# Expert products of a pair in unbroken runs, and tiles placed by the width of the matmuls that read them

## The chip, the cores and the metric

The kernel runs on one core of a Trainium2 chip. The metric is device time in microseconds of one execution; the median of several runs counts. The core's engines work from queues of their own: TensorE (PE, matmuls, with its weight loads as PEld), VectorE (DVE), ScalarE (ACT), GpSimd (POOL) and SyncE (SP), which issues the transfers here.

## What is computed

A network of three blocks on 512 tokens of width 1024. Two blocks (the loop over `l`) each hold stick-breaking attention, differential attention, a gated merge, a mixture of 32 experts and a gated addition of a side input; the third (`hybrid`, `ffn`) holds dilated, block-wise and recurrent branches and a dense feed-forward part. The change bears on the expert part:

```python
def expert_block(args):                    # a block of the tokens sent to expert e
    xb, e = args
    hid = jax.nn.silu(xb @ w_gate[e]) * (xb @ w_up[e])
    return hid @ w_down[e]
ys = lax.map(expert_block, (xs, blk_e)).reshape(P, D)
ys = ys * slot_gate[:, None]               # each token goes to two experts
out = jax.ops.segment_sum(ys, slot_tok, num_segments=N + 1)[:N]
```

## The kernel before

**Dense matmuls.** A float32 product is made of three float32r matmuls (high x high, high x low, low x high; `mm3`, lines 269 to 274). `wload` and `wcut` (242 to 259) load 512 KB of weights into a tile of tag `raw` and split it into two tiles of tag `wh`. `proj_f` streams 512 columns of the normalised activations (tag `f16`) against stationary `wh`; `add_out` and the end of `ffn` stream 256 columns of `wh` against stationary tiles of `q`, `o`, `g` or `tmp`; `proj_v` and others stream `wh` against stationary `f16`.

**Places.** A pool lays its tags out one after the other, in the order of their first use; all buffers of a tag follow one another. In each partition the tiles of `q`, `raw`, `wh` and `o` begin at a multiple of 128 bytes, and those of `tmp`, `f16`, `g`, `X` and `wu` 64 bytes past one.

**The expert stage** (`moe`, 908 to 1180, once for each `l`). Experts go in groups of two, 64 token places each: 16 groups, and a 17th with one expert more. A step is two matmuls side by side, one for each expert, in either half of TensorE's columns (64 of 128), each in plain float32. Group g has 8 steps `up` (gate and up product) and 4 steps `dn` (down product). The list `steps` is up 0, up 1, dn 0, up 2, dn 1 and so on, one entry a step. Other pieces are put between steps by `at(s, ...)`, in full-width matmuls or transposes:

- `gather_oh(u, tt)` (983): VectorE writes a slice of the one-hot tile OH(u) (tag `g`) for groups 2u and 2u+1; four slices, two operations each;
- `gather_rows(u, kk)` (1014): 16 matmuls that select rows, into a PSUM tile `z`, then a copy into X(u); `gather_gates(u)` (996): 8 small matmuls into `tp`, then five small VectorE operations;
- `back(u, p)` (1028): four transposes of OH(u) into `tp`, copied to OHT(u) (tag `g`);
- `hidden(g)` (1051): two transposes of the hidden values into `tp`, and a copy that `dn` g reads;
- `combine` (1070): four matmuls of OHT with the split product rows Y (tag `q`) into the one PSUM tile `o`, then an addition on VectorE that empties it; 56 of them, for 7 pairs of groups, 4 token tiles and 2 halves.

A piece that ends in an evacuation returns a function, which is put into the step after (lines 1160 to 1163). After `up`, `gate` runs on ScalarE and VectorE; after `dn`, `rows` copies on ScalarE and subtracts on VectorE. `manual_schedule` (1158) keeps the order as written in each queue of PE, ACT, DVE and POOL. Tags have fixed numbers of buffers: in this stage `g` has 4, `X` 2, `wu` (incoming weights) 5; of PSUM, `z` and `mm` have 2, `tp` and `o` have 1. A tile that finds no free buffer makes its first writer wait until the last reader of another one has ended.

In these indices, with 12 steps a group, OH(u) is written at steps 24u-25 to 24u-22 and last read at 24u-5; OHT(u) is written at 24u-6 and 24u-4 and read by additions up to step 24u+54.

Of the kernel before, what the change touches and what calls it, by code (L numbers as in the profile page):

```python
# [22 lines left out]
EARLY = dict(then=0, rope=-30, cut=20, norm=0, trans=0, route=0, fold=0, y=0, gather=0, hs=0, dma=0)  # L23
RAW, WHL, NWU = 4, 6, 5
HT = 4
LM, LH, LF = 1, 1, 3

GAT = (-25, -24, -23, -22, -9, -15, -13, -11, -9)
BAT = (-7, -5)
CAT = (40, 2)  # L30
ROPE_FREQ = (1.0, 0.1939227432012558, 0.03760603070259094, 0.007292664609849453, 0.0014142135623842478,
# [76 lines left out]
class Kern:  # L108
    def __init__(self, ctx, tc, A, out, dbg=None, stop=None):
        self.tc, self.nc, self.A, self.out = tc, tc.nc, A, out  # L110
        self.dbg, self.stop = dbg or {}, stop
        self.n = 0
        self.const = ctx.enter_context(tc.tile_pool(name="const", bufs=1))
        self.sb = ctx.enter_context(tc.tile_pool(name="sb", bufs=1))
        self.ps = ctx.enter_context(tc.tile_pool(name="ps", bufs=1, space=PSUM))
        self.dr = ctx.enter_context(tc.tile_pool(name="dr", bufs=1, space=bass.MemoryType.DRAM))
        self.ph = None
        ctx.callback(lambda: self.ph.close())
        self.phase("mix")
# [4 lines left out]
    def phase(self, name):  # L124

        if self.ph is not None:
            self.ph.close()
        self.ph = ExitStack()
        self.n += 1
        self.phsb = self.ph.enter_context(self.tc.tile_pool(name=f"{name}{self.n}", bufs=1, reuse_waits="tile"))  # L130
        self.phbufs = dict(self.PHASES[name])

    def ring(self, tag, shape, dt):

        return self.t(tag, shape, dt, bufs={"raw": RAW, "wh": WHL}[tag])


    def t(self, tag, shape, dt=F32, bufs=None):
        self.n += 1
        if tag in self.phbufs:  # L140
            return self.phsb.tile(shape, dt, tag=tag, name=f"{tag}_{self.n}", bufs=self.phbufs[tag])
        return self.sb.tile(shape, dt, tag=tag, name=f"{tag}_{self.n}", bufs=bufs)
# [98 lines left out]

    def wload(self, src, a, b, eH="act", eL="dve"):
# [4 lines left out]
        return self.wcut(raw, a, b, eH, eL)  # L247

# [3 lines left out]

    def wcut(self, raw, a, b, eH="act", eL="dve"):

        h, l = (self.ring("wh", [128, a, b], F32R) for _ in range(2))
# [219 lines left out]
    def proj_v(self, hT, w, cols, r):  # L475

        wc = [self.wload(self.wk(w, cols, kh), 4, 256) for kh in range(2)]
        for tp in range(2):
# [13 lines left out]
    def proj_f_halves(self, hT, w, c0, r):  # L492

        r += [self.mmps([128, S]) for _ in range(2)]
        wc = [self.wload(self.wk(w, c0, kh), 4, 256) for kh in range(2)]
        for half in range(2):
# [411 lines left out]
    def moe(self, l, xs):  # L908
# [9 lines left out]
        for g, tags in ((0, ("raw", "raw", "wh", "wh")), (1, ("q",) * 4)):  # L918
            for c in range(4):
                for i in range(2):  # L920
                    t = self.t(tags[c], [128, 2, 2, 256], F32, bufs={"raw": RAW, "wh": WHL, "q": 12}[tags[c]])
# [7 lines left out]
        for g in range(NG + 1):  # L929
            if g < NG:  # L930
                up[g] = len(steps)
                steps += [("up", g, j) for j in range(4 * ne(g))]
            if g > 0:
                if g == NG:
                    steps += [None] * 2
                dn[g - 1] = len(steps)
                steps += [("dn", g - 1, j) for j in range(2 * ne(g - 1))]
        N = len(steps)
# [17 lines left out]
        def load_in():  # L956
            if way_in:
# [4 lines left out]
                for k in range(4):  # L962
                    IN[g, i, 4 * h + k] = t[:, :, k]
                free = up[g] + (4 * h + 3 if ne(g) == 2 else 2 * h + 1)
                loads.setdefault(free, []).append(load_in)

        def load_out():
            if way_out:
                g, k, i = way_out.pop(0)
                tag = out_tags[nout[0] % 10]  # L970
                nout[0] += 1
                t = OUT[g, i, k] = self.t(tag, [128, 1024], F32, bufs={"raw": RAW, "wh": WHL}[tag])
                nc.sync.dma_start(t, weights(g, i)[2][k * 128:k * 128 + 128])
                loads.setdefault(dn[g] + (2 * k + 1 if ne(g) == 2 else 1), []).append(load_out)

# [38 lines left out]
        def gather_rows(u, kk):  # L1014
# [80 lines left out]
        def work(s):  # L1095

            kind, g, j = steps[s]
            two = ne(g) == 2
            if kind == "up":
                if j == 0:  # L1100
                    PS["a", g] = self.mmps([128, 2, 256])
                pa, X = PS["a", g], Xs[g // 2]
                for i in range(2):
                    k, e = (j, i) if two else (2 * j + i, 0)
                    x0 = (g % 2 * 2 + e) * 64
                    mm(pa[64 * i:64 * i + 64], X[:, k, x0:x0 + 64], IN.pop((g, e, k)), start=j == 0, stop=j == 4 * ne(g) - 1)
                if j == 4 * ne(g) - 1:
                    if two:
                        at(s + 1, lambda: gate(g, 0))
                        at(s + 2, lambda: gate(g, 1))  # L1110
                    else:
                        at(s + 1, lambda: folded("a", g, pa.rearrange("p j c -> p (j c)"),
                                                 lambda: (gate(g, 0), gate(g, 1))))
                    at(max(s + 4, dn[g] - HT), lambda: hidden(g))
            else:
                if j == 0:
                    PS["y", g] = self.pst("z", [128, 1024], 2)
                py = PS["y", g]
                for i in range(2):
                    k, q, e = (j // 2, j % 2, i) if two else (i, j, 0)  # L1120
                    cs = slice(q * 512, q * 512 + 512)
                    mm(py[64 * i:64 * i + 64, cs], HID[g][:, k, 64 * e:64 * e + 64], OUT[g, e, k][:, cs],
                       start=k == 0 or not two, stop=k == 1 or not two)
                if j == 2 * ne(g) - 1:
                    if two:
                        at(s + 1, lambda: rows(g, 0))
                        at(s + 2, lambda: rows(g, 1))
                    else:
                        at(s + 1, lambda: folded("y", g, py, lambda: (rows(g, 0), rows(g, 1))))
            for f in loads.pop(s, ()):  # L1130
                f()

        for u in range(1, 9):
            for tt in range(4):
                at(24 * u + GAT[tt], lambda u=u, tt=tt: gather_oh(u, tt))
            at(24 * u + GAT[4], lambda u=u: gather_gates(u))
            for kk in range(4):
                at(24 * u + GAT[5 + kk], lambda u=u, kk=kk: gather_rows(u, kk))
        for u in range(9):
            for p in range(2 if u < 8 else 1):  # L1140
                at(max(24 * u + BAT[p], 2 + p), lambda u=u, p=p: back(u, p))
        for j in range(7):
            for x in range(8):
                at(min(CAT[0] + 24 * j + CAT[1] * x, N + x - 8), lambda j=j, x=x: combine((2 * j, 2 * j + 1), x // 2, x % 2))
        self.moe_overflow(l, xs, hs, G, it, oe)
# [9 lines left out]
        gather_gates(0)()  # L1155
        self.moe_blocks(oe, it)
        ET = mybir.EngineType
        with self.tc.manual_schedule(engines={ET.PE, ET.Activation, ET.DVE, ET.Pool}):
            for s in range(N + 8):
                for f in todo.pop(s, ()):  # L1160
                    f = f()
                    if callable(f):
                        at(s + 1, f)
                if s in (3, 7) and s < N:
                    for _ in range(4):
                        loads.setdefault(s, []).append(load_out)
                if s < N and steps[s]:
# [139 lines left out]
    def ple(self, l, xs, then=None):  # L1307
# [3 lines left out]
        for c in range(4):  # L1311
            wc = [self.wload(self.wk(A["w_ple_gate"][l], c * 256, kh), 4, 256) for kh in range(2)]
            for tt in range(4):
# [136 lines left out]
    def dilated(self, hT, w):  # L1450
# [4 lines left out]
        for g in range(3):  # L1455
# [11 lines left out]
            for kh in range(2):  # L1467
                wc = self.wload(self.wk(w, 1536 + g * 256, kh), 4, 256)
                for tt in range(4):
# [377 lines left out]
```

## Time and profile before

| | |
|---|---|
| median of 3 runs | 2871.1 us (2870.6 to 2871.26) |
| the profiled execution | 2876.8 us, span 2875.1 us |
| TensorE busy / weight loads | 2716.9 us (94%) / 2025.3 us (70%) |
| VectorE, ScalarE, GpSimd busy | 1379.6 us (48%), 969.4 us (34%), 318.6 us (11%) |
| granted clock, mean | 0.967 of 2.4 GHz |
| moved | 383.57 MB, mean 133 GB/s |

The share of busy time is a mean over stages; the windows show single ones. Rows of the lines view give busy time and count of a group of like instructions, the mean of one, and the engine's idle time before them with what ended it. A timeline row is a series of like instructions with its start. A matmul's own duration overlaps the next one's, so work is read from starts to starts. A float32 matmul stands as two instructions in it, so a step of an expert product counts 4.

### The profile page before, as it was taken

Reading aid. Unit: us, or ns where it says so; the run is one execution under the profiler, and the core shown is the slowest. Engines: PE = TensorE matmul, PEld = TensorE weight load, DVE = VectorE, ACT = ScalarE, POOL = GpSimd, SP = SyncE. Lnnn points to the kernel's source line nnn. Section 1 sums busy time; section 2 is a strip of 40 time slices with the busy share of each in tenths; the row PEclk is TensorE's granted clock in tenths of the full one; section 3 lists DMA queues with packets and bytes.
Section 4 is the critical chain, followed back from the end, with each engine's and each line's share of the span. In section 5 each row is a group of like instructions: output and inputs, shape, how many; then the busy total and the mean of one; then the engine's idle time right before and its main releaser. Section 6 shows DMA issues by size and latency. Waiting matters only on the chain.

```text
span 2875.1 us, 37304 instructions
## 1 busy us (share of the span) xinstructions
PE 2716.9 (94%) x14791; PEld 2025.3 (70%) x14791; DVE 1379.6 (48%) x2585; ACT 969.4 (34%) x1752; POOL 318.6 (11%) x346
## 2 busy tenths in 40 slices
PE   7899996999999999999699999899999899999998
PEld 6777785544558777789444546877886677877798
DVE  6677536233347567643633336654235812533323
ACT  4555322111124445532111114544343622322222
POOL 0221001000000022010100000210001543011101
PEclk9989997999999989999799999999999999999999
DMA  5112234788853211133688872322112233233222
GB/s 170 45 37 74 81 120 150 292 302 289 294 192 103 74 45 52 59 98 123 222 312 287 296 289 96 118 74 66 52 45 70 74 99 114 81 95 96 91 90 70
DMA packets 224771, 383.57 MB, mean 133 GB/s; under 512 B 19658, under 2 KB 162599, under 8 KB 224592
## 3 DMA queue, kind: packets, MB, share of 16 engines
q1 hardware_dynamic: 224592, 381.13, 39.7%
q8 instruction: 119, 1.95, 0.3%
q14 instruction: 60, 0.49, 0.1%
HBM read 374.23 MB, written 6.85 MB: 133 GB/s over the span
## 4 chain that ended last, share of the span: by engine, by line
PE 44%; DVE 4%; ACT 1%; POOL 1%; issue 1%; POOLq 0%; DVEq 0%; ACTq 0%
PE mm L272 8%; PE mm L274 8%; PE mm L273 8%; PE z L911 5%; PE mm L911 4%; PE o L911 2%; PE z L272 1%; PE z L274 1%; PE z L273 1%; PE o L524 1%; DVE tmp L345 1%; PE o L1440 1%; PE z L1429 0%; PE z L1427 0%; DVE tmp L1595 0%
## 5 line engine op out<-in xcount | busy, mean ns | idle before, releaser
L240 DVE TENSOR_TENSOR wh<-raw,wh 128x1024 fp32r<-128x1024 f32 (+1 forms) x251 | 304.2, 1214 | 476.6 <-ACT wh L227 474.3
L272 PE MATMUL mm<-f,wh 128*128 128x512 f32 x1264 | 508.0, 404 | 3.2 <-DVE q L238 2.1
L273 PE MATMUL mm<-f,wh 128*128 128x512 f32 x1264 | 508.0, 402 | 0.0
L274 PE MATMUL mm<-f,wh 128*128 128x512 f32 x1264 | 506.5, 401 | 0.1
L227 ACT ACTIVATE wh<-raw 128x1024 fp32r<-128x1024 f32 (+1 forms) x278 | 290.4, 1046 | 505.8 <-PE mm L273 350.1
L272 PEld LDWEIGHTS mm<-f,wh 128*128 128x128 f32 x1264 | 239.7, 190 | 66.9 <-issue 6.3
L274 PEld LDWEIGHTS mm<-f,wh 128*128 128x128 f32 x1264 | 240.2, 190 | 56.5 <-issue 2.0
L273 PEld LDWEIGHTS mm<-f,wh 128*128 128x128 f32 x1264 | 240.1, 190 | 54.3 <-issue 2.2
L911 PE MATMUL mm<-wu,X 128*64 128x512 f32 x928 | 229.2, 606 | 0.0
L911 PEld LDWEIGHTS z<-g,o 128*128 128x128 f32 x1152 | 141.2, 192 | 51.0 <-issue 14.6
L911 PE MATMUL z<-g,o 128*128 128x256 f32 (+1 forms) x1152 | 154.2, 288 | 10.8 <-DVE g L994 10.8
L911 PEld LDWEIGHTS o<-q,g 128*128 128x128 f32 x448 | 75.4, 188 | 104.4 <-issue 56.8
L484 PE MATMUL mm<-wh,f 128*128 128x256 f32 x960 | 137.8, 297 | 6.0 <-ACT f L386 3.1
L911 PE MATMUL o<-q,g 128*128 128x512 f32 x448 | 134.7, 422 | 3.3 <-DVE q L1078 3.3
L484 PEld LDWEIGHTS mm<-wh,f 128*128 128x128 f32 x960 | 127.3, 200 | 11.5 <-ACT f L386 4.8
L1078 DVE TENSOR_TENSOR q<-q,o 128x512 f32<-128x512 f32 x112 | 76.6, 684 | 108.7 <-PE o L911 108.7
L911 PEld LDWEIGHTS mm<-wu,X 128*64 128x64 f32 x928 | 55.5, 136 | 87.3 <-issue 79.2
L272 PE MATMUL mm<-wh,q 128*128 128x256 f32 x384 | 112.1, 292 | 3.7 <-ACT q L227 3.7
L274 PE MATMUL mm<-wh,q 128*128 128x256 f32 x384 | 110.0, 286 | 2.4 <-POOL q L240 2.2
L273 PE MATMUL mm<-wh,q 128*128 128x256 f32 x384 | 109.3, 285 | 0.0
L273 PE MATMUL mm<-wh,f 128*128 128x256 f32 x352 | 106.1, 301 | 0.8 <-DVE wh L240 0.8
L274 PE MATMUL mm<-wh,f 128*128 128x256 f32 x352 | 106.0, 301 | 0.6 <-DVE f L387 0.6
(432 smaller groups left out, 4732.7 us busy)
## 6 DMA issues: line engine op xcount, KB each, us to landing
raw<-in_w_in_dram SPq DMA_DIRECT2D x142, 512.0 KB, 3.6
wu<-in_w_exp_gate_dram SPq DMA_DIRECT2D x116, 512.0 KB
wu<-in_w_exp_up_dram SPq DMA_DIRECT2D x116, 512.0 KB, 8.4
wh<-in_w_exp_down_dram SPq DMA_DIRECT2D x76, 512.0 KB, 6.2
raw<-in_w_exp_down_dram SPq DMA_DIRECT2D x56, 512.0 KB, 6.1
raw<-in_w_gu_dram SPq DMA_DIRECT2D x44, 512.0 KB, 3.4
raw<-in_w_down_dram SPq DMA_DIRECT2D x20, 512.0 KB, 3.5
raw<-in_w_o_dram SPq DMA_DIRECT2D x16, 512.0 KB, 5.2
```

Of the source, the lines that this page charges most:

```text
L227: nc.scalar.activation(o, i, AF.Copy, scale=scale)
L240: e.tensor_sub(o, i, h)
L272: mm(ps, aH, bH, start=first, stop=False, skip_group_check=True)
L273: mm(ps, aH, bL, start=False, stop=False, skip_group_check=True)
L274: mm(ps, aL, bH, start=False, stop=last, skip_group_check=True)
L345: self.nc.vector.scalar_tensor_tensor(h.rearrange("t k p -> t p k"), x.rearrange("t (p k) -> t p k", k=8), r, gb.rearrange("t (p k) -> t p ...
L484: self.nc.tensor.matmul(ps[:, t], hT[k // 4][:, x, k % 4, sl], wc[k // 4][y][:, k % 4], start=t + x + y + k == 0, stop=x == 1 and k == 7, ...
L524: self.nc.tensor.matmul(po, v[kt // 2][:, x, kt % 2, vc], w[y][:, kt, :], start=x + y + kt == 0, stop=y == 1 and kt == nk - 1, skip_group_ ...
L911: mm = lambda *a, **k: nc.tensor.matmul(*a, **k, skip_group_check=True)
L1078: return lambda: v.tensor_add(xs[tt][:, cs], xs[tt][:, cs], po)
L1440: nc.tensor.matmul(po[:, m, qt % 2], v[:, qt - prev + j, vc], pT[:, m, j], start=m == 0 and j == 0 and qt % 2 == 0, stop=j == prev, skip_g ...
```

## The change

1. **Runs.** An entry of `steps` is a whole product: all steps of `up` g, or of `dn` g, follow one another. The list has 35 entries (before 201): up g is step 2g-1, dn g is 2g+2. Pieces stand between products, and evacuations come right behind their matmuls, no longer a step later.
2. **Places in the list.** In one step: gates first, then the first half's `combine`, gathers and transposes, the second half's `combine`, then one-hot slices. OH(u) is written in steps 4u-6 and 4u-5; gathers of u are in 4u-4 to 4u-1, its transposes in 4u-2 and 4u-1; additions for groups 2u and 2u+1 in 4u+6 to 4u+9. All copies into X go to ScalarE.
3. **Places in memory.** Pads move tags: then `q` and `g` begin 64 bytes past a multiple of 128, and `raw`, `o`, `tmp`, `f16` at one. `wh` has slots of 4608 bytes and begins at a multiple, or 64 past one (`skip=64`) where it streams against `f16` or in `proj_f_halves`.
4. **Buffers.** `wu` has 6; the scratch for GpSimd's transfers (none are issued there) falls from 16 KB to 1 KB a partition.

```diff
-RAW, WHL, NWU = 4, 6, 5
+RAW, WHL, NWU = 4, 6, 6
...
+    def ring(self, tag, shape, dt, skip=0):
+        if tag == "raw":
+            return self.t(tag, shape, dt, bufs=RAW)
+        o = skip // 4
+        t = self.t(tag, [128, 1152], dt, bufs=WHL)[:, o:o + int(np.prod(shape[1:]))]
...
+    PADS = {("sb", "q"): 320, ("sb", "raw"): 192, ("mix", "tmp"): 64, ("mix", "f16"): 256, ("mix", "g"): 320, ("moe", "g"): 128}
     def t(self, tag, shape, dt=F32, bufs=None):
         self.n += 1
+        pad = self.PADS.get((self.phname if tag in self.phbufs else "sb", tag), 0)
+        if pad and (tag in self.phbufs, tag) not in self.padded:
+            self.padded.add((tag in self.phbufs, tag))
+            pool = self.phsb if tag in self.phbufs else self.sb
+            self.nc.gpsimd.memset(pool.tile([128, pad // 4], F32, name=f"pad_{self.n}")[:, 0:1], 0.0)
...
-        wc = [self.wload(self.wk(w, cols, kh), 4, 256) for kh in range(2)]
+        wc = [self.wload(self.wk(w, cols, kh), 4, 256, skip=64) for kh in range(2)]
...
-                steps += [("up", g, j) for j in range(4 * ne(g))]
+                steps.append(("up", g))
             if g > 0:
                 if g == NG:
-                    steps += [None] * 2
+                    steps.append(None)
                 dn[g - 1] = len(steps)
-                steps += [("dn", g - 1, j) for j in range(2 * ne(g - 1))]
+                steps.append(("dn", g - 1))
...
-            return lambda: self.copyH(Xs[u][:, kk * 2:kk * 2 + 2, 0:n], pz[:, :, 0:n], "act" if kk % 2 == 0 else "dve")
+            return lambda: nc.scalar.copy(Xs[u][:, kk * 2:kk * 2 + 2, 0:n], pz[:, :, 0:n])
...
+                n = 4 * ne(g)
+                for j in range(n):
+                    for i in range(2):
+                        k, e = (j, i) if two else (2 * j + i, 0)
+                        x0 = (g % 2 * 2 + e) * 64
+                        mm(pa[64 * i:64 * i + 64], X[:, k, x0:x0 + 64], IN.pop((g, e, k)), start=j == 0, stop=j == n - 1)
+                    for f in loads.pop((s, k), ()):
+                        f()
+                if two:
+                    gate(g, 0)
+                    gate(g, 1)
...
+                at(max(s + 2, dn[g] - 1) + (not two), lambda: hidden(g))
...
+        for u in range(1, 9):
+            at(max(4 * u - 3, 1), lambda u=u: gather_gates(u))
+        def back_rows(y):
+            for j in range(7):
+                for x in range(4):
+                    at(min(4 * j + 6 + x, N), lambda j=j, x=x: combine((2 * j, 2 * j + 1), x, y))
+        back_rows(0)
+        for u in range(9):
+            for x in range(4):
+                if u:
+                    at(max(4 * u - 4 + x, 1), lambda u=u, x=x: gather_rows(u, x))
+                if x < 2 and 2 * u + x < NG:
+                    at(max(4 * u - 2 + x, 1 + x), lambda u=u, x=x: back(u, x))
+        back_rows(1)
         for u in range(1, 9):
             for tt in range(4):
-                at(24 * u + GAT[tt], lambda u=u, tt=tt: gather_oh(u, tt))
...
+                at(4 * u - 6 + tt // 2, lambda u=u, tt=tt: gather_oh(u, tt))
...
                 for f in todo.pop(s, ()):
                     f = f()
                     if callable(f):
-                        at(s + 1, f)
+                        f()
...
-    nc = _bacc.Bacc("TRN2", target_bir_lowering=False, num_devices=1)
+    nc = _bacc.Bacc("TRN2", target_bir_lowering=False, num_devices=1, dynamic_dma_scratch_size=1024)
```

## Rows read from the trace of the kernel before

**Rows 1.** Busy time of each engine (the page's first part).
```profile
PE 2716.9 (94%) x14791; PEld 2025.3 (70%) x14791; DVE 1379.6 (48%) x2585; ACT 969.4 (34%) x1752; POOL 318.6 (11%) x346
```

**Rows 2.** Windows: stretch, length, busy PE PEld DVE ACT POOL, PEclk, DMA share, GB/s.
```profile
600.00:700.00 100.00, 100.00 (x504) 49.58 (x500) 33.25 (x70) 13.74 (x24) 0.00 (x0) 1.00 0.82 285
```

**Rows 3.** Waits, 500 to 860 us: engine, line, releaser: total, times, longest.
```profile
PEld tp L1036 <- ACT g L1037: 0.8, 1, 0.8
...
PE o L911 <- DVE q L1078: 1.6, 1, 1.6
```

**Rows 4.** Waits of SyncE's queue in the same stretch.
```profile
SPq L961 <- PE mm L911: 149.9, 27, 7.5
```

**Rows 5.** TensorE's timeline in the first expert stage: start, busy, line, tiles, count.
```profile
509.24 0.66 PE L1036 MATMUL tp<-c_all,g 128*128 128x128 f32 x4
...
512.33 3.60 PE L911 MATMUL mm<-wh,X 128*64 128x512 f32 x16
515.76 1.03 PE L911 MATMUL mm<-q,X 128*64 128x512 f32 x4
...
662.17 1.21 PE L911 MATMUL o<-q,g 128*128 128x512 f32 x4
663.31 1.94 PE L911 MATMUL mm<-wu,X 128*64 128x512 f32 x8
665.18 1.21 PE L911 MATMUL o<-q,g 128*128 128x512 f32 x4
...
848.11 1.19 PE L911 MATMUL z<-q,g 128*128 128x512 f32 x4
```

**Rows 6.** VectorE's timeline: start, busy, line, operation, tiles, [idle before].
```profile
660.30 1.23 DVE L240 TENSOR_TENSOR q<-z,q 128x1024 fp32r<-128x1024 f32 x1 [3.01 <-ACT q L227]
661.44 0.68 DVE L1078 TENSOR_TENSOR q<-q,o 128x512 f32<-128x512 f32 x1
...
664.03 0.35 DVE L993 TENSOR_SCALAR g<-c_all,small 128x256 fp32r<-128x256 f32 x1
...
664.81 0.35 DVE L993 TENSOR_SCALAR g<-c_all,small 128x256 fp32r<-128x256 f32 x1
```

**Rows 7.** TensorE's timeline at two waits, and a window behind each.
```profile
2289.07 0.50 PE L272 MATMUL mm<-o,wh 128*128 128x512 f32 x1 [3.24 <-ACT o L227]
...
2434.43 0.58 PE L272 MATMUL mm<-wh,q 128*128 128x256 f32 x1 [3.69 <-ACT q L227]
...
2289.50:2292.90 3.40, 3.18 (x8) 2.51 (x8) 2.67 (x4) 1.61 (x3) 2.34 (x1) 0.51 0.01 3
2432.80:2439.60 6.80, 5.05 (x22) 4.75 (x23) 0.42 (x1) 1.14 (x3) 2.18 (x2) 0.50 0.25 81
```

**Rows 8.** TensorE's timeline: first and last of four unbroken series.
```profile
2321.11 0.39 PE L272 MATMUL mm<-o,wh 128*128 128x512 f32 x1
...
2331.79 0.39 PE L274 MATMUL mm<-o,wh 128*128 128x512 f32 x1
2332.02 0.39 PE L272 MATMUL mm<-f,wh 128*128 128x512 f32 x1
...
2365.39 0.39 PE L274 MATMUL mm<-f,wh 128*128 128x512 f32 x1
...
2800.63 0.28 PE L272 MATMUL z<-wh,q 128*128 128x256 f32 x1
...
2812.03 0.28 PE L274 MATMUL z<-wh,q 128*128 128x256 f32 x1
...
2823.67 0.28 PE L272 MATMUL z<-wh,g 128*128 128x256 f32 x1
...
2828.99 0.28 PE L274 MATMUL z<-wh,g 128*128 128x256 f32 x1
```

**Rows 9.** Costliest groups (the page's fifth part): tiles and counts of two.
```profile
L272 PE MATMUL mm<-f,wh 128*128 128x512 f32 x1264 | 508.0, 404 | 3.2 <-DVE q L238 2.1
...
L272 PE MATMUL mm<-wh,q 128*128 128x256 f32 x384 | 112.1, 292 | 3.7 <-ACT q L227 3.7
```

More of the change, by code (lines that the diff above doesn't have):

```diff
@@ L23 @@
 EARLY = dict(then=0, rope=-30, cut=20, norm=0, trans=0, route=0, fold=0, y=0, gather=0, hs=0, dma=0)
-RAW, WHL, NWU = 4, 6, 5
-HT = 4
+RAW, WHL, NWU = 4, 6, 6
 LM, LH, LF = 1, 1, 3
-GAT = (-25, -24, -23, -22, -9, -15, -13, -11, -9)
-BAT = (-7, -5)
-CAT = (40, 2)
 ROPE_FREQ = (1.0, 0.1939227432012558, 0.03760603070259094, 0.007292664609849453, 0.0014142135623842478,
@@ L116, in __init__ @@
         self.dr = ctx.enter_context(tc.tile_pool(name="dr", bufs=1, space=bass.MemoryType.DRAM))
-        self.ph = None
+        self.ph, self.padded = None, set()
         ctx.callback(lambda: self.ph.close())
@@ L130, in phase @@
         self.phsb = self.ph.enter_context(self.tc.tile_pool(name=f"{name}{self.n}", bufs=1, reuse_waits="tile"))
-        self.phbufs = dict(self.PHASES[name])
-    def ring(self, tag, shape, dt):
-        return self.t(tag, shape, dt, bufs={"raw": RAW, "wh": WHL}[tag])
+        self.phbufs, self.phname = dict(self.PHASES[name]), name
+        self.padded = {x for x in self.padded if not x[0]}
+    def ring(self, tag, shape, dt, skip=0):
[3 more added lines that the diff above has]
+        t = self.t(tag, [128, 1152], dt, bufs=WHL)[:, o:o + int(np.prod(shape[1:]))]
+        return t if len(shape) == 2 else t.rearrange({3: "p (a b) -> p a b", 4: "p (a b c) -> p a b c"}[len(shape)],
+                                                     **dict(zip("ab", shape[1:-1])))
+    PADS = {("sb", "q"): 320, ("sb", "raw"): 192, ("mix", "tmp"): 64, ("mix", "f16"): 256, ("mix", "g"): 320, ("moe", "g"): 128}
     def t(self, tag, shape, dt=F32, bufs=None):
         self.n += 1
+        pad = self.PADS.get((self.phname if tag in self.phbufs else "sb", tag), 0)
[3 more added lines that the diff above has]
+            self.nc.gpsimd.memset(pool.tile([128, pad // 4], F32, name=f"pad_{self.n}")[:, 0:1], 0.0)
         if tag in self.phbufs:
@@ L240, in subL, with wload @@
             e.tensor_sub(o, i, h)
-    def wload(self, src, a, b, eH="act", eL="dve"):
+    def wload(self, src, a, b, eH="act", eL="dve", skip=0):
         raw = self.ring("raw", [128, a, b], F32)
@@ L246, in wload, with wcut @@
             self.nc.sync.dma_start(raw if d is None else raw[:, :, d], ap)
-        return self.wcut(raw, a, b, eH, eL)
+        return self.wcut(raw, a, b, eH, eL, skip)
     def early(self, what):
         return self.tc.high_priority(EARLY[what])
-    def wcut(self, raw, a, b, eH="act", eL="dve"):
-        h, l = (self.ring("wh", [128, a, b], F32R) for _ in range(2))
+    def wcut(self, raw, a, b, eH="act", eL="dve", skip=0):
+        h, l = (self.ring("wh", [128, a, b], F32R, skip) for _ in range(2))
         with self.early("cut"):
@@ L494, in proj_f_halves @@
         r += [self.mmps([128, S]) for _ in range(2)]
-        wc = [self.wload(self.wk(w, c0, kh), 4, 256) for kh in range(2)]
+        wc = [self.wload(self.wk(w, c0, kh), 4, 256, skip=64) for kh in range(2)]
         for half in range(2):
@@ L920, in moe @@
                 for i in range(2):
-                    t = self.t(tags[c], [128, 2, 2, 256], F32, bufs={"raw": RAW, "wh": WHL, "q": 12}[tags[c]])
+                    t = self.F4([128, 2, 2, 256], tag="q") if tags[c] == "q" else self.ring(tags[c], [128, 2, 2, 256], F32)
                     for j, w in enumerate((wg, wu)):
@@ L963, in load_in @@
                     IN[g, i, 4 * h + k] = t[:, :, k]
-                free = up[g] + (4 * h + 3 if ne(g) == 2 else 2 * h + 1)
-                loads.setdefault(free, []).append(load_in)
+                loads.setdefault((up[g], 4 * h + 3), []).append(load_in)
         def load_out():
@@ L971, in load_out @@
                 nout[0] += 1
-                t = OUT[g, i, k] = self.t(tag, [128, 1024], F32, bufs={"raw": RAW, "wh": WHL}[tag])
+                t = OUT[g, i, k] = self.ring(tag, [128, 1024], F32)
                 nc.sync.dma_start(t, weights(g, i)[2][k * 128:k * 128 + 128])
-                loads.setdefault(dn[g] + (2 * k + 1 if ne(g) == 2 else 1), []).append(load_out)
+                loads.setdefault((dn[g], 2 * k + 1), []).append(load_out)
         self.phase("moe")
@@ L1095, in work @@
         def work(s):
-            kind, g, j = steps[s]
+            kind, g = steps[s]
             two = ne(g) == 2
             if kind == "up":
[L1100 to L1114, printed above, removed]
-            else:
[L1116 to L1129, printed above, removed]
@@ L1130, in work @@
-            for f in loads.pop(s, ()):
-                f()
+                pa, X = self.mmps([128, 2, 256]), Xs[g // 2]
+                PS["a", g] = pa
+                n = 4 * ne(g)
[6 more added lines that the diff above has]
+                        f()
@@ new lines, in work @@
+                if two:
+                    gate(g, 0)
+                    gate(g, 1)
+                else:
+                    at(s + 1, lambda: folded("a", g, pa.rearrange("p j c -> p (j c)"), lambda: (gate(g, 0), gate(g, 1))))
+                at(max(s + 2, dn[g] - 1) + (not two), lambda: hidden(g))
+            else:
+                py = PS["y", g] = self.pst("z", [128, 1024], 2)
+                n = 2 * ne(g)
+                for j in range(n):
+                    for i in range(2):
+                        k, q, e = (j // 2, j % 2, i) if two else (i, j, 0)
+                        cs = slice(q * 512, q * 512 + 512)
+                        mm(py[64 * i:64 * i + 64, cs], HID[g][:, k, 64 * e:64 * e + 64], OUT[g, e, k][:, cs],
+                           start=k == 0 or not two, stop=k == 1 or not two)
+                    for f in loads.pop((s, j), ()):
+                        f()
+                if two:
+                    rows(g, 0)
+                    rows(g, 1)
+                else:
+                    at(s + 1, lambda: folded("y", g, py, lambda: (rows(g, 0), rows(g, 1))))
@@ L1133, in moe @@
+        back_rows(1)
         for u in range(1, 9):
             for tt in range(4):
-                at(24 * u + GAT[tt], lambda u=u, tt=tt: gather_oh(u, tt))
[L1136 to L1144, printed above, removed]
+                at(4 * u - 6 + tt // 2, lambda u=u, tt=tt: gather_oh(u, tt))
@@ L1156, in moe @@
         self.moe_blocks(oe, it)
+        for k in (3, 7):
+            loads.setdefault((0, k), []).extend([load_out] * 4)
         ET = mybir.EngineType
@@ L1162, in moe @@
                     if callable(f):
-                        at(s + 1, f)
-                if s in (3, 7) and s < N:
-                    for _ in range(4):
-                        loads.setdefault(s, []).append(load_out)
+                        f()
                 if s < N and steps[s]:
@@ L1311, in ple @@
         for c in range(4):
-            wc = [self.wload(self.wk(A["w_ple_gate"][l], c * 256, kh), 4, 256) for kh in range(2)]
+            wc = [self.wload(self.wk(A["w_ple_gate"][l], c * 256, kh), 4, 256, skip=64) for kh in range(2)]
             for tt in range(4):
@@ L1467, in dilated @@
             for kh in range(2):
-                wc = self.wload(self.wk(w, 1536 + g * 256, kh), 4, 256)
+                wc = self.wload(self.wk(w, 1536 + g * 256, kh), 4, 256, skip=64)
                 for tt in range(4):
```

## The prediction

> **What bounds the kernel now.** I read the busy shares first: TensorE works for 94% of the span and every other engine for half of it or less [rows 1]. So a change counts where TensorE's own order, its spacing or its waits change. Next, the two expert stages, 507 to 849 us and 1412 to 1752 us, by windows: TensorE is 100% busy at a granted clock of 1.00 [rows 2]. Its waits there are nearly nothing: one of 1.6 us on an addition is the longest [rows 3]. SyncE's queue on the contrary waits for TensorE: 149.9 us of this stage for buffers that matmuls still read [rows 4]. So transfers are held back by TensorE, not the reverse, and each expert stage is as long as TensorE's instruction list. Outside these stages, long rows of float32r matmuls fill the engine, and the spacing of their starts is what counts.
>
> **Sum to be made against.** The profiled execution took 2876.8 us, span 2875.1; the median of the runs is 2871.1. All terms below are differences in TensorE's time, so I add them to the median.
>
> **1. Runs (gain).** A pair's product is two half-width matmuls side by side. Four steps in a row with nothing between take 515.76 - 512.33 = 3.43 us, 0.858 a step [rows 5]. Two steps between two other pieces take 665.18 - 663.31 = 1.87, that is 0.15 more than 1.716. The addition's four matmuls take 663.31 - 662.17 = 1.14 where 4 x 0.233 [rows 8] = 0.93 would do: 0.21 more. So leaving half-width work and coming back costs 0.36 us with an addition between. For a gather or transpose between I have the 0.15 as floor and 0.36 as top, and take 0.31, since part of what surrounds it is the same return. In a layer TensorE leaves half-width work 114 times: I counted them in its timeline, the first at 509.24 and the last at 848.11 [rows 5]; 55 of them go to an addition. With runs there are 17 products in and 17 out, so 33 departures, 28 to an addition (steps 6 to 33) and 5 to something else. Removed: 27 x 0.36 + 54 x 0.31 = 26 us a layer.
>
> Against it stand short new waits, since evacuations and their readers now come closer. The one buffer of the transposes is shared by gates, row selectors and hidden values: in steps 1 to 5 it has some 1.5, 0.9, 0.9, 0.6 and 0.5 us of such waits (a chain of small VectorE operations or a ScalarE copy each time), the additions after a gates step 0.25 us six times, the last ones 3 us, less the 2.2 us that the kernel has now: together 7.5 us. Lower bound 0, upper 12. **Net of runs: -18.5 us a layer.**
>
> **2. One-hots (loss).** This is the term that decides. All one-hot tiles (OH, four 256-wide slices for a pair of groups u) and all transposed ones (OHT) share the tag g, with 4 buffers. After the change OH(u) is written in steps 4u-6 and 4u-5 and read until the gather in step 4u-1. OHT(u) is written in steps 4u-2 and 4u-1 and read by additions until step 4u+9. In step 4u-2, then, OHT(u-2), OHT(u-1), OHT(u) and OH(u) are all alive when OH(u+1) is to be written: five tiles for four buffers. Before, OH(u+1) was written from step 24u-1 on, after OH(u)'s last read at 24u-5, and nothing waited.
>
> The order in each engine's queue is fixed as written, and a piece may wait for one that stands later on another engine: that happens once now, where a transpose waits for the ScalarE copy written after it [rows 3]. So VectorE stops at the first slice of OH(u+1) until the last gather of OH(u), in the next step, has ended. Behind it in VectorE's queue stand: three more operations for the one-hots, then the subtraction that splits the last product, then the first addition of step 4u-1. TensorE does that step's first addition matmuls, the transposes and the gather, and then needs the one PSUM bank "o", which that addition has to empty. From the end of the gather: two slices 2 x 0.78 (664.03 to 664.81 is one slice), the subtraction 661.44 - 660.30 = 1.14, the addition 0.68 [rows 6], and some 0.3 us for the gather's own end and the signals: 3.7 us. Nothing covers it, since TensorE's next piece is queued behind. It happens for u+1 = 3 to 8 (u+1 = 2 still finds a free buffer): **6 x 3.7 = +22 us a layer**. No row excludes 0 (a buffer I count as taken is free); top 24.
>
> **3. Clock (loss).** After an isolated wait of 3.69 us TensorE's granted clock is 0.50 for 6.8 us, after one of 3.24 us it is 0.51 for 3.4 us [rows 7]. These are its lower level, 1.2 of 2.4 GHz; in an expert stage, with no such wait, it is 1.00 [rows 2]. In the first case 5.2 us of the slow stretch lie behind the wait and in the second all 3.4 us: 2.6 and 1.7 us of work lost. In the changed kernel a dense run of eight steps follows each wait, so I take 2.0 us, bounds 0.7 and 3.0: **6 x 2.0 = +12 us a layer**.
>
> **4. Placement (gain).** The offset of a tile within 128 bytes matters. 143 intervals of 512-wide matmuls with moving operand f16 (64 past a multiple) and weights wh (on one) take 2365.39 - 2332.02 = 33.37 us, 233.3 ns each; 47 with moving o (on one, as the weights) take 10.68 us, 227.2 ns [rows 8]. With 256-wide ones it is the other way: wh against q, both on a multiple, 95 intervals in 11.40 us, 120.0 ns; wh against g, 64 apart, 47 in 5.32 us, 113.2 ns [rows 8]. The pads bring f16 to a multiple of 128, as wh is, and q to 64 past one. There are 3 x 1264 of the first kind and 3 x 384 beside 288 in the last stage of the second [rows 9]. In short series the 512-wide gap shows little, so I count 2,700 x 6.5 ns = 17.5 us. For wh against q I take two thirds of 6.8 ns, since only the stationary tag differs from the g series: 1,400 x 4.5 ns = 6.3 us, bounds 0 and 9.5. Losses: the 96 against tmp and 96 f16 against o go the wrong way, 1.2 us. Of 22.6 us I book **-20 us in all**, as a little ends in waits for ScalarE and VectorE; bounds 10 and 27.
> The page "TensorE: Matmul & The Clock Gate" of the Trainium skill (Part 2, step 1 of its step-by-step list) says that the engine has two independent read ports and that loading the next weights takes no read bandwidth from the running matmul. By that rule the place of a tile changes nothing and the sum has no such term; the rows above do not agree with it.
>
> **Edits at nothing.** The pad writes are one column each on GpSimd, 11% busy [rows 1]. The selected rows' copies all go to ScalarE (0.6 us each, under a product or the next gather). A sixth weight buffer and the smaller scratch change no wait of TensorE, as it waits for no transfer now; if that cover goes, rival E prices it.
>
> **Sum.** 2871.1 + 2 x (-18.5 + 22 + 12) - 20 = 2882 us, 0.4% slower. With the ends of the terms, combined: 2858 to 2902.
>
> **Rivals.**
> A, the forecast: 2882 us, chance 0.55.
> B, the one-hots don't wait, because one of the five tiles isn't alive or the order lets the additions pass. For it: only that the count of five comes from steps, not from a trace. Against it: the buffers of g are 4 and full today too. Terms 2 and 3 vanish: 2871 - 37 - 20 = 2814, chance 0.20. The point at which it decides is one buffer of g: with five tiles in four, A; with four alive, B.
> C, the wait is there but the clock stays at its upper level, as it did over the one wait of 1.6 us [rows 3]: 2871 + 7 - 20 = 2858, chance 0.12.
> D, placement brings nothing (the rule on read ports beside term 4), the waits are as in A: 2902, chance 0.08.
> E, the runs are as in B but transfers become the bound. A pair needs 6.29 MB; at the 285 GB/s of [rows 2] that is 22 us against 20 us of TensorE work, so only the placement is left: 2871 - 20 = 2851, chance 0.05. Against it: SyncE waits for TensorE today [rows 4].
>
> **How the numbers follow.** I predict 2882. A's own range is 2858 to 2902. As the cases of both signs hold much, 8 in 10 needs B as well: 2808 to 2900. About 0.2% (5.7 us) is what a measurement of this kernel tells from no change. Faster by more than that: B, E, most of C and a little of A, 0.38; within: the rest of C and A's lower part, 0.14; slower: 0.48.
>
> **What would show it.** Right: in each expert stage TensorE's departures fall from 114 to about 33; six idle times of some 3.7 us before an addition's matmuls (tile "o"), put down to an addition; VectorE idle before a one-hot slice, released by the gather on TensorE; windows of clock 0.5 behind each; 512-wide f16 series at 227 ns and wh against q at 113 to 118. Wrong: expert stages of some 322 us with no wait for VectorE (B), the waits at clock 1.00 (C), series still at 233 ns (D), or weight loads that wait for a transfer (E).

## The result and the profile after

The changed kernel takes 2889.0 us (median of 5 runs, 2885.7 to 2894.0) beside 2871.3 for the kernel before in the same session: ratio 1.0053, 95% interval 1.0041 to 1.0064 (the two medians alone give 1.0062, inside it). It is 0.5% slower. 2882 was forecast, in a range from 2808 to 2900.

The profiled execution took 2885.7 us, span 2883.8. Its windows of the first expert stage, of two stretches behind waits, and the columns as in [rows 2]:

```profile
505.20:859.00 353.80, 327.40 (x1690) 177.09 (x1686) 104.45 (x222) 59.22 (x102) 0.00 (x0) 0.96 0.71 260
...
617.90:621.30 3.40, 3.40 (x10) 1.96 (x12) 1.36 (x4) 0.37 (x1) 0.00 (x0) 0.50 0.01 2
...
706.60:713.40 6.80, 6.31 (x16) 2.85 (x18) 2.62 (x6) 0.37 (x1) 0.00 (x0) 0.50 0.07 26
```

Where the stage was 100% busy at clock 1.00 [rows 2], it now has 26 us without TensorE and two lengths of stretches at half clock. From the first half-width matmul to the last it takes 354.9 us, before 340.2; in the second layer 355.0 and 340.2. TensorE leaves half-width work 35 times in it, before 114 times. So the runs are there; something else has taken more than they gave. The waits of the same stage name it (engine, line, tile, releaser: total, times, longest):

```profile
DVE g L1002 <- PE z L921: 37.6, 6, 6.3
...
PE o L921 <- DVE q L1087: 23.5, 8, 3.5
```

VectorE waits six times to write a one-hot slice (line 1002, tile g) until a gather on TensorE (tile z) has ended, and TensorE waits for an addition on VectorE (line 1087) to empty "o"; six of these eight waits are 3.48 us long, and the other two, of 0.78 and 1.86 us, stand at the end of the stage. Before, VectorE had no such wait, and TensorE waited for the addition (line 1078 there) once, 1.6 us [rows 3]. One of the six, first on TensorE and then on VectorE (start, busy, line, tiles, idle before):

```profile
611.86 0.60 PE L1045 MATMUL tp<-c_all,g 128*128 128x128 f32 x4
612.22 2.13 PE L921 MATMUL z<-g,o 128*128 128x256 f32 x16
617.83 2.04 PE L921 MATMUL o<-q,g 128*128 128x512 f32 x4 [3.48 <-DVE q L1087]
```

```profile
614.38 0.35 DVE L1002 TENSOR_SCALAR g<-c_all,small 128x256 fp32r<-128x256 f32 x1 [6.26 <-PE z L921]
614.77 0.48 DVE L1003 SCALAR_TENSOR_TENSOR g<-c_all,small,g 128x256 fp32r<-128x256 f32 x1
615.17 0.35 DVE L1002 TENSOR_SCALAR g<-c_all,small 128x256 fp32r<-128x256 f32 x1
615.56 0.49 DVE L1003 SCALAR_TENSOR_TENSOR g<-c_all,small,g 128x256 fp32r<-128x256 f32 x1
615.96 1.22 DVE L250 TENSOR_TENSOR q<-z,q 128x1024 fp32r<-128x1024 f32 x1
617.09 0.68 DVE L1087 TENSOR_TENSOR q<-q,o 128x512 f32<-128x512 f32 x1
```

Read together: the gather ends at 614.35, and VectorE, idle for 6.26 us, starts its slice at 614.38. Two slices, the subtraction and the addition later, "o" is free, and TensorE goes on at 617.83. That is the queue of [rows 6], one behind the other. The next stretch, from 617.90, runs at 0.50.

Outside the expert stages the long series are faster, as forecast: the same 143 intervals as in [rows 8] take 2382.45 - 2350.03 = 32.42 us, 226.7 ns each (before 233.3).

```profile
2350.03 0.39 PE L282 MATMUL mm<-f,wh 128*128 128x512 f32 x1
...
2382.45 0.39 PE L284 MATMUL mm<-f,wh 128*128 128x512 f32 x1
...
2808.59 0.28 PE L282 MATMUL z<-wh,q 128*128 128x256 f32 x1
...
2819.78 0.28 PE L284 MATMUL z<-wh,q 128*128 128x256 f32 x1
...
2831.42 0.28 PE L282 MATMUL z<-wh,g 128*128 128x256 f32 x1
...
2836.96 0.28 PE L284 MATMUL z<-wh,g 128*128 128x256 f32 x1
```

A trap lies here. The two profiled spans differ by 8.7 us and the expert stages by 29.5, so the rest of this pair of profiles gained 20.8, just the 20 of term 4. But the medians differ by 17.7 us: the profiled execution of before lies 5.5 above its median, and that of after 3.3 below. By medians the rest gained 11.8. Experiment 4 decides between the two.

### The profile page after: what moved, and what is told of

Read it like the earlier page. It is cut to its first block, busy times and chain, and to the rows that moved or that the text cites. A ratio compares the mean times of both kernels' runs of the same rounds, so it can differ in the third digit from the quotient of the medians.

```text
span 2883.8 us, 37301 instructions
## 1 busy us (share of the span) xinstructions
PE 2668.5 (93%) x14791; PEld 2040.7 (71%) x14791; DVE 1351.1 (47%) x2549; ACT 987.7 (34%) x1788; POOL 319.8 (11%) x357
## 4 chain that ended last, share of the span: by engine, by line
PE 42%; DVE 6%; ACT 1%; POOL 1%; issue 1%; POOLq 0%; DVEq 0%; ACTq 0%
PE mm L282 8%; PE mm L284 7%; PE mm L283 7%; PE z L921 5%; PE mm L921 4%; PE o L921 2%; PE z L283 1%; PE z L282 1%; PE z L284 1%; PE o L534 1%; DVE tmp L355 1%; PE o L1454 1%; PE z L1443 0%; DVE wh L250 0%; PE z L1441 0%
## 5 line engine op out<-in xcount | busy, mean ns | idle before, releaser
L282 PE MATMUL mm<-f,wh 128*128 128x512 f32 x1264 | 503.4, 400 | 3.2 <-DVE q L248 2.0
L283 PE MATMUL mm<-f,wh 128*128 128x512 f32 x1264 | 500.3, 396 | 0.0
L284 PE MATMUL mm<-f,wh 128*128 128x512 f32 x1264 | 499.6, 396 | 0.1
L921 PE MATMUL mm<-wu,X 128*64 128x512 f32 x928 | 218.6, 625 | 0.0
L921 PEld LDWEIGHTS mm<-wu,X 128*64 128x64 f32 x928 | 66.7, 145 | 132.3 <-issue 130.6
L921 PEld LDWEIGHTS z<-g,o 128*128 128x128 f32 x1152 | 146.4, 194 | 15.9 <-DVE g L1003 11.8
L494 PE MATMUL mm<-wh,f 128*128 128x256 f32 x960 | 135.3, 293 | 6.7 <-ACT f L396 3.7
L1057 DVE SCALAR_TENSOR_TENSOR gs<-gs,mm 128x256 f32<-128x256 f32 x32 | 13.5, 421 | 220.9 <-ACT gs L441 220.9
L282 PE MATMUL mm<-wh,q 128*128 128x256 f32 x384 | 110.0, 287 | 3.7 <-ACT q L237 3.7
L284 PE MATMUL mm<-wh,q 128*128 128x256 f32 x384 | 108.1, 281 | 2.8 <-POOL q L250 2.8
L283 PE MATMUL mm<-wh,q 128*128 128x256 f32 x384 | 107.2, 280 | 0.0
L283 PE MATMUL mm<-wh,f 128*128 128x256 f32 x352 | 106.2, 302 | 0.6 <-DVE wh L250 0.6
```

The costliest lines, as they stand in the source:

```text
L282: mm(ps, aH, bH, start=first, stop=False, skip_group_check=True)
L283: mm(ps, aH, bL, start=False, stop=False, skip_group_check=True)
L284: mm(ps, aL, bH, start=False, stop=last, skip_group_check=True)
L494: self.nc.tensor.matmul(ps[:, t], hT[k // 4][:, x, k % 4, sl], wc[k // 4][y][:, k % 4], start=t + x + y + k == 0, stop=x == 1 and k == 7, ...
L921: mm = lambda *a, **k: nc.tensor.matmul(*a, **k, skip_group_check=True)
L1057: v.scalar_tensor_tensor(sg[r], sg[r], 1.0, pa[r, 0], op0=OP.add, op1=OP.mult)
```

## The experiments

In what follows, times in microseconds from ratios are ratio differences times 2871, since the runs came in several sessions.

**1. The fifth tile.** First the order: all slices of OH(u) in step 4u-5, behind the last gather of OH(u-1).

```diff
-                at(4 * u - 6 + tt // 2, lambda u=u, tt=tt: gather_oh(u, tt))
+                at(4 * u - 5, lambda u=u, tt=tt: gather_oh(u, tt))
```

> The changed kernel with one edit: all four slices of OH(u) are written in step 4u-5, behind the last gather of OH(u-1), instead of two slices in step 4u-6 and two in 4u-5. Then at most four tiles of tag g are alive. Theory 1 (the fifth tile makes VectorE wait, the waits pull the clock down): the 12 waits of 3.48 us (6 a layer) and the half-clock windows behind them (five of 3.4 us and one of 6.8 us a layer, half of each lost, 11.9 us) go: 2889 - 2 x (20.9 + 11.9) = 2823 us, 2815 to 2832, granted clock 1.00 within the expert stages. Rival 2 (the waits come from evacuations packed between products, not from the buffer): waits before the second-half additions stay, 2880 to 2890. Rival 3 (transfers become the bound once TensorE stops waiting): weight loads wait for transfers, some 2850 us.

Measured: 2822.4 us, ratio 0.9820 (0.9806 to 0.9833), against 2823 by the theory of the fifth tile. VectorE no longer waits for a gather before a one-hot slice; of TensorE's waits for an addition the two at the end of the stage are left, and its weight loads wait for transfers 1.5 us in all (from 500 to 860 us; the lines on z and tp count further down):

```profile
PE o L921 <- DVE q L1087: 2.7, 2, 1.9
PE z L921 <- ACT hid L1067: 1.2, 2, 0.7
...
PEld mm L921 <- DMA raw<-in_w_exp_down_dram: 1.0, 5, 0.3
...
PE tp L1045 <- DVE small L1015: 0.9, 1, 0.9
...
PE tp L1045 <- ACT g L1046: 0.7, 1, 0.7
...
PEld mm L921 <- DMA wh<-in_w_exp_down_dram: 0.5, 3, 0.2
```

The stages take 319.4 and 320.5 us, while the transfers go at 289 GB/s, more than the 285 of [rows 2]:

```profile
505.20:823.10 317.90, 312.27 (x1688) 171.85 (x1684) 103.91 (x221) 59.23 (x102) 0.00 (x0) 1.00 0.78 289
```

Then the buffer, with the order of the changed kernel untouched:

```diff
-RAW, WHL, NWU = 4, 6, 6
+RAW, WHL, NWU = 4, 6, 5
...
-    PHASES = {"mix": dict(tmp=7, g=4, f16=2, reset=1), "moe": dict(y=1, gs=2, g=4, X=2, hid=2, wu=NWU)}
+    PHASES = {"mix": dict(tmp=7, g=4, f16=2, reset=1), "moe": dict(y=1, gs=2, g=5, X=2, hid=2, wu=NWU)}
```

> The changed kernel with the order untouched, but five buffers for tag g in the expert stage and five instead of six for the incoming weights, which pays for them. Theory 1: a fifth buffer holds the fifth tile, the waits go as in the kernel with late one-hots, 2823 us, 2815 to 2832. Rival 2 (the order itself, not the buffer): 2880 to 2890. Rival 3 (the sixth weight buffer is what keeps TensorE fed): slower than the kernel with late one-hots by 5 us or more, with waits of TensorE for transfers.

Measured: 2824.6 us, ratio 0.9829 (0.9813 to 0.9845), stages of 320.2 and 319.3 us, and the same two waits left:

```profile
PE o L921 <- DVE q L1087: 2.6, 2, 1.9
```

Two unlike cures, a later write and one more buffer, give the same time. So the cause is the number of buffers of g against the tiles alive, and not the order as such. The sixth weight buffer, missing here, is worth nothing that these intervals can show.

**2. The length of the wait.** One slice and four slices in step 4u-6, where the changed kernel has two.

```diff
-                at(4 * u - 6 + tt // 2, lambda u=u, tt=tt: gather_oh(u, tt))
+                at(4 * u - 6 + (tt > 0), lambda u=u, tt=tt: gather_oh(u, tt))   # one slice
+                at(4 * u - 6, lambda u=u, tt=tt: gather_oh(u, tt))              # or: four slices
```

> The changed kernel, but only the first slice of OH(u) stays in step 4u-6; three go to step 4u-5. Theory 1 (the wait is the sum of VectorE's queue behind the freed buffer): the 12 waits shrink by one slice, 0.79 us, from 3.48 to 2.69 us; if the half-clock windows behind them stay as in the changed kernel (11.9 us lost a layer), 2889 - 12 x 0.79 = 2880 us. If a wait of 2.69 us no longer pulls the clock down, also 24 us less: 2856. Rival (only whether there is a wait matters, or its length is set by something else): waits of 3.4 to 3.5 us, 2887 to 2891.

> The changed kernel, but all four slices of OH(u) in step 4u-6. Theory 1: the 12 waits grow by two slices, from 3.48 to 5.06 us; with the windows at half clock as in the changed kernel 2889 + 12 x 1.58 = 2908 us; if most windows grow from 3.4 to 6.8 us, up to 2928. Rival: waits stay at 3.4 to 3.5 us, 2887 to 2891.

Measured: with one slice 2875.7 us, ratio 1.0002 (0.9993 to 1.0011), with four 2915.5 us, ratio 1.0147 (1.0131 to 1.0162). One of the waits in each, first with one slice, then with four:

```profile
618.02 1.20 PE L921 MATMUL o<-q,g 128*128 128x512 f32 x4 [2.69 <-DVE q L1087]
```

```profile
622.74 2.08 PE L921 MATMUL o<-q,g 128*128 128x512 f32 x4 [5.05 <-DVE q L1087]
```

The wait is what VectorE has queued behind the freed buffer, to a hundredth of a microsecond: 2.69, 3.48, 5.05, a slice being 0.79. The clock is the rest of the difference: with four slices the stages are 13.6 and 11.3 us longer than in the changed kernel, 9.4 of them wait, and with one 7.8 and 9.7 us shorter, 4.7 of them wait. With one slice the stretches at half clock behind these waits last 3.4 us, and one wait in each layer is followed by none; with two there are five of 3.4 us and one of 6.8 in a layer, with four five of 6.8 and one of 3.4. So the first forecast (2880) is some 5 us too high, and the second (2908 to 2928) holds.

**3. The price of the clock.** The waits stay, but TensorE is given 13 matmuls to do meanwhile. This is added work; its product is not read.

```diff
+        def filler(g):
+            t = self.mmps([128, 512])
+            for _ in range(13):
+                mm(t, OHT[g][:, 0:128], Y[g][0][:, 0:512], start=True, stop=True)
...
                 for x in range(4):
+                    if y == 1 and x == 1 and j < 6:
+                        at(4 * j + 7, lambda j=j: filler(2 * j))
```

> The changed kernel with the 12 waits left as they are, but TensorE does 13 more matmuls of 512 columns (some 3.0 us, added work whose product nobody reads, into a free buffer of tag mm) ahead of the addition that waits for 3.48 us. Theory (the half-clock windows come from TensorE standing still and cost 11.9 us a layer): some 0.5 us of each wait is left, no time is lost by the added matmuls, and the granted clock stays at 1.00 through the expert stages: 2889 - 2 x 11.9 = 2865 us, 2860 to 2870. Rival C (the windows have another cause, or cost nothing): 2885 to 2893.

Measured: 2866.1 us, ratio 0.9976 (0.9966 to 0.9985), against 2865. VectorE waits as before (37.6 us, 6 times), the addition comes no sooner, TensorE has 13 matmuls more to do at each place, and the kernel is 22 us faster than the changed one:

```profile
614.47 3.12 PE L921 MATMUL mm<-q,g 128*128 128x512 f32 x13
618.12 1.20 PE L921 MATMUL o<-q,g 128*128 128x512 f32 x4 [0.53 <-DVE q L1087]
```

```profile
505.20:842.00 336.80, 330.39 (x1764) 185.80 (x1763) 100.95 (x223) 57.09 (x100) 0.00 (x0) 1.00 0.73 273
```

The granted clock is 1.00 up to the last waits of the stage. So the half clock follows from TensorE standing still, and by the ratios costs 11 us a layer; rival C is out. By the traces the two stages are 10.9 and 13.0 us shorter than in the changed kernel; in the second the half-clock stretch at the end of the stage is gone too. The page "TensorE: Matmul & The Clock Gate" of the Trainium skill (Part 1, "HAM oscillation — how this bites in real kernels") reckons the loss as half of the throttled time; by it the 29.3 us a layer at half clock in the changed kernel, less the 5.3 and 0 in this one, cost 12 and 15 us, an estimate a little above the 10.9 and 13.0 of the traces.

**4. Places alone, and the changes without them.** The kernel before with pads, slots, offsets and the smaller scratch; the changed kernel without pads, slots and offsets; the kernel of experiment 1 without them. Of the first edit, one line:

```diff
...
+    PADS = {("sb", "q"): 320, ("sb", "raw"): 192, ("mix", "tmp"): 64, ("mix", "f16"): 256, ("mix", "g"): 320, ("moe", "g"): 128}
...
```

> The kernel before with the places in memory alone (pads, slots of 4608 bytes and their 64-byte offset, smaller scratch); lists of steps, five weight buffers and pieces as before. Theory 1: long series with 512 moving columns of f16 go from 233 to 227 ns, 256-wide wh against q from 120 to 113-118 ns: 2871 - 20 = 2851 us, 2844 to 2861. Rival (placement brings nothing, the gains outside the expert stages in the changed kernel are chance of the clock): 2869 to 2873.

> The changed kernel without its places (no pads, wh slots of 4096 bytes without offset); runs, step list, six weight buffers as changed. Theory 1: the expert stages keep their 12 waits, the series outside go back to 233 and 120 ns: 2889 + 20 = 2909 us, 2899 to 2916. If placement brings nothing: 2887 to 2891. If the places also matter inside the expert stages, the stage lengths differ from the 356 us of the changed kernel by more than 3 us.

> The kernel with late one-hots without its places in memory. Placement alone gave 6.7 us on the kernel before and 10.3 on the changed one. Theory 4 (the series outside the expert stages get faster by some 20 us in all, but only those of the last stage, where TensorE is the bound, shorten the run; elsewhere the gain turns into waits): 2822 + 7 to 10 = 2829 to 2832. If the -20 of the prediction holds without the other changes' waits: 2842. Stage by stage, the last block should lose 9 us or more and the stages before it little.

Measured: 2864.8 us, ratio 0.9965 (0.9951 to 0.9978); 2899.3 us, ratio 1.0087 (1.0073 to 1.0101); 2833.6 us, ratio 0.9859 (0.9844 to 0.9874). Placement is so worth 0.0035, 0.0034 and 0.0039, that is 10, 10 and 11 us on three kernels that differ in the rest. So it brings something (rival D doesn't hold, nor the conclusion, drawn beside term 4 from the rule on read ports, that the place of a tile changes nothing), but half of the 20. Where the other half is can be read from two stretches with the same matmuls in the kernel before and in the one with places alone; first from behind the first expert stage to the second one (the attention of the second layer), then the dense part of the last block:

```profile
884.58:1413.89 529.31, 481.63 (x2830) 402.65 (x2828) 321.57 (x595) 216.34 (x378) 63.86 (x100) 0.94 0.30 94
2276.93:2769.55 492.62, 479.51 (x2402) 400.08 (x2401) 164.68 (x210) 144.59 (x204) 108.86 (x64) 0.99 0.31 95
```

```profile
881.10:1409.82 528.72, 479.44 (x2831) 404.92 (x2829) 319.86 (x595) 216.54 (x378) 64.47 (x100) 0.93 0.29 95
2273.36:2756.22 482.86, 468.48 (x2402) 396.54 (x2400) 164.86 (x210) 144.77 (x204) 108.94 (x64) 0.99 0.31 97
```

In the last block TensorE is busy for 97%, and its two longest waits are those of [rows 7]: busy time falls by 11.0 us, and the stretch by 9.8. Over the attention it is busy for 91%, waits for other engines and falls to half clock after such waits: busy time falls by 2.2 us, and the stretch by 0.6. There, 657 intervals of f16 against wh became shorter (233.3 to 228.3 ns, 3.3 us by starts), but TensorE only came sooner to the next wait, and at half clock somewhat longer (0.93 after 0.94). Over the three pairs of kernels the dense stretch gains 8.4 to 10.6 us each time, and the attention stretch between -2.8 and +1.2; in the pair with -2.8 it has 20 us more at half clock. The two other stretches outside the expert stages lie between: 1.0 to 3.6 us up to the first stage, 0.8 to 6.0 from the second stage to the dense part. So outside the dense part single profiles differ by as much as placement gives; in sum the three stretches there gain 3 to 8 us.

**5. The price of leaving a run.** The first-half additions are put into the middle of the product before; everything else as in experiment 1.

```diff
+                    if j == n // 2 - 1:
+                        middle(s)
...
+                    if y == 0 and s < N and steps[s - 1]:
+                        inside[s - 1] = f
+                    else:
+                        at(s, f)
```

`middle(s)` runs what `inside` holds for step s, after half the steps of its product.

> The kernel with late one-hots (2822 us), but the first-half additions (28 a layer, four matmuls each) are put into the middle of the product before instead of behind it. It computes the same with the same instructions; TensorE leaves half-width work 28 times more in a layer. Theory (a departure and return costs 0.31 to 0.36 us): 2822 + 2 x 28 x 0.31 to 0.36 = 2840 to 2842 us, expert stages of some 343 us, no new wait. Rival (the gain of the runs is not in the departures but in copies, buffers or prefetch): 2820 to 2825.

Measured: 2827.8 us, ratio 0.9842 (0.9829 to 0.9855): 6 us more than experiment 1 where 18 to 20 were forecast. TensorE leaves half-width work 62 times a layer in place of 35, and the stages take 323.7 us each, against 319.4 and 320.5. The trace of the first layer says why it is so little: intervals between an addition's matmuls, or from a gather to an addition, sum to 45.6 us (194 of them) in place of 50.5 (196); without the two that are gone, at 0.23 us each, that is 4.4 less. An addition inside a product finds "o" already emptied, and the waits at the end of the stage (2.7 us above) are gone. So 27 departures more cost 4.4 + 4.4 = 8.8 us, 0.33 each, inside the 0.31 to 0.36; this split is an estimate from starts in the trace, and no run shows it by itself. The next run takes the other half of it, the waits, alone.

**6. Only the last three additions inside.**

```diff
...
+                    if y == 0 and j == 6 and x:
+                        inside[s - 1] = f
...
```

> The kernel with late one-hots (2822 us), with only the last three first-half additions of a layer put into the middle of the product before. In the late kernel these last additions wait 3.2 us a layer for VectorE, and one wait of 1.9 us is followed by a half-clock window in one of the layers. Theory: -3.2 us and 3 x 0.35 us for three more departures, so some -2 us a layer, and up to 2 us for the window: 2816 to 2819 us. Rival (the waits move to the next addition): 2821 to 2825.

Measured: 2817.3 us, ratio 0.9805 (0.9792 to 0.9819), stages of 316.8 us in both layers: with three departures more, the stages are 2.6 and 3.7 us shorter (in the second a half-clock stretch of 3.4 us is gone too), and no wait of TensorE for an addition is left. By the intervals it can't be told from experiment 1 as a whole; it is some 2% faster than the kernel before and 2.5% faster than the changed one.

## Why the prediction was right

**The step that decided held.** Term 2 put five tiles into four buffers, six waits a layer of 3.7 us before an addition, VectorE idle before a one-hot slice, released by the gather. There are six a layer, of 3.48 us, at just these places. The 0.2 us between are the signals: they take less than the 0.3 us that I had added. Together the six take 20.9 us a layer (22 forecast).

**The clock** was put at 12 us a layer, from two waits outside the expert stages [rows 7]. Experiment 3 gives 11. Waits and clock together, from the difference to experiment 1 (1.0053 - 0.9820), cost 33.4 us a layer against 34; the two measured apart, 20.9 and 11, make 31.9.

**The runs** were put at -18.5 us a layer net. Experiment 1 less the kernel with places alone gives 0.9820 - 0.9965, 41.6 us in all, -20.8 a layer. There are 35 departures for the 33 forecast; 22 and not 28 go to an addition, since gates stand first in six of those steps, which hardly changes the sum. The short waits are mis-sized: those that term 1 lists add up to 6.7 us and not 7.5, and in experiment 1 TensorE's waits in the stage sum to 5.5 us (2.7, 1.2, 0.9 and 0.7) where it had 1.6 before, 3.9 more. That leaves 20.8 + 3.9 = 24.7 us for 79 departures less, 0.31 each: an estimate that fits the price of term 1.

**Placement** is the term that was mis-sized: -20 forecast, -10 measured, the lower bound. The interval of the series was right (226.7 for 227 ns; 117.8 for 113 to 118). Summed by starts over the whole kernel, places alone shorten the intervals of f16 against wh by some 21 us and those of wh against q by 5.5, where 17.5 and 6.3 were counted (at 6.5 ns, where [rows 8] give 233.3 - 227.2 = 6.1; and the short series, which term 4 left out, have the gap as well). What failed is the sentence that "a little ends in waits for ScalarE and VectorE": about half of it does. I counted the matmuls of all stages alike, though windows of the attention would have shown TensorE busy for 91% with the clock at 0.94 there; that share of the series should have been put at less than half.

With the measured terms: 2871 + 2 x (-20.8 + 33.4) - 10 = 2886. This is no test of the terms, as all three are differences along one chain of kernels and must add up to the measured ratio, 1.0053 x 2871. With waits and clock measured apart (31.9) it is 2883, against 2889. That 2882 came as near as it did is luck in part: placement, 10 us too large, and the runs, 4.6 us too small, err in opposite directions.

**The rivals.** B is the time of a kernel without the wait, and experiment 1 shows what it would have been: 2822, not 2814; the 8 us between are mostly placement (10 us), less what the runs gave more. E did not come: without the waits transfers went at 289 GB/s over the stage, and TensorE's weight loads waited 1.5 us for them. Its price took every pair to be moved within the stage; 289 GB/s over 317.9 us are 92 MB, that is at most 14.6 of the 16.5 pairs.

## What to carry to other kernels

When a list of work is made coarser, tiles live for longer in it: count those of each tag that are alive at each step against its buffers before putting a write into a step, and read off which queue stands behind the write that would wait. In this kernel's expert stages, otherwise at full clock, waits of 3.48 us cost half as much again behind them (11 us on 20.9), so that even throw-away matmuls in the wait paid. And a faster matmul is worth its nanoseconds where TensorE is the bound: multiply by the count in those stages, and expect half or less elsewhere, as here.

## What the runs showed that I had not expected

The distance of two tiles modulo 128 bytes is not the whole rule for 256 columns. wh against g stands 64 apart in both kernels; 47 intervals took 5.32 us before, 113.2 ns [rows 8], and 2836.96 - 2831.42 = 5.54 us after, 117.9 ns, as much as wh against q in the last stage after the change (117.8). The slot of wh, 4608 bytes for 4096, can't be the whole reason: in the changed kernel a series of wh against q earlier in the last block, with the same slots, takes 2490.64 - 2455.96 = 34.68 us for 306 intervals, 113.3 ns each.

```profile
2455.96 0.28 PE L282 MATMUL mm<-wh,q 128*128 128x256 f32 x1
...
2490.64 0.28 PE L282 MATMUL mm<-wh,q 128*128 128x256 f32 x1
```

What decides between the two values stays open.

Waits of nearly one length did not all have the same sequel. After 2.69 us the clock fell in five of six cases in each layer, after some 1.87 us at the end of the stage in some layers and not in others (for 6.8 us in both layers of the changed kernel, and in one layer, for 3.4 us, in experiment 1). Even the wait of 1.6 us over which the clock of the kernel before stayed up [rows 3] is no safe case: with places alone it lasts 1.67 us, and in the second layer the clock falls behind it, in the first not.

```profile
1745.93 0.50 PE L926 MATMUL o<-q,g 128*128 128x512 f32 x1 [1.67 <-DVE q L1093]
```

```profile
1747.42:1750.83 3.41, 3.41 (x9) 0.91 (x6) 2.70 (x3) 1.46 (x3) 0.00 (x0) 0.51 0.00 0
```

What decides between them stays open.
